# Gate projections of blocks 1 to 7: two blocks at a time in seven half-size products instead of eight

## The chip, the cores and the metric

The kernel runs on one core of a Trainium2 chip. The time is the device time of one execution in microseconds (us). Three runs of the kernel before took 754.03, 754.44 and 754.73 us. Engines: TensorE (PE, matmuls; its weight loads are shown apart as PEld), VectorE (DVE), ScalarE (ACT), GpSimd (POOL), and SyncE (SP), which issues the DMAs here. Each engine takes its instructions strictly in its own queue's order and waits at semaphores.

## The reference

A transformer block on 512 tokens of width 1024 in float32. After a normalization, one big projection gives the inputs of four mixers and, for each of them, a gate of full width:

```python
h = rmsnorm(x, norm_mix_pre[l])
(c_q, c_kv, k_r, sg_u, sg_v, cv_x, cv_b, cv_c, pool_in, gate_pre) = split_cols(h @ w_in[l])
gates = jax.nn.sigmoid(gate_pre + gate_b[l]).reshape(B_, S_, N_BRANCH, D_)
y_a = mla(...) @ w_br_mla[l]                  # attention
y_b = spatial_gating(...) @ w_br_sg[l]
y_c = short_conv(...) @ w_br_conv[l]
y_d = multiscale_pool(...) @ w_br_pool[l]
merged = (gates[:, :, 0] * y_a + gates[:, :, 1] * y_b
          + gates[:, :, 2] * y_c + gates[:, :, 3] * y_d)
x = x + rmsnorm(merged @ w_out[l], norm_mix_post[l])
h = rmsnorm(x, norm_ffn_pre[l])
f = jnp.square(jax.nn.relu(h @ w_ff1[l])) @ w_ff2[l]
x = x + rmsnorm(f, norm_ffn_post[l])
```

gate_pre has 4 x 1024 columns, so the gates are a product of [512, 1024] with [1024, 4096].

## The kernel before

Every float32 product is made of three matmuls: both operands are split into a high and a low half in a reduced-precision float32 format, and `mm3` (L119) adds hi x hi, hi x lo and lo x hi in PSUM. Weights come by DMA into a `raw` tile (three buffers, L105), ACT casts them to `wh` and DVE subtracts to get `wl` (L109 to L114; five buffers each). The activations z = x * g are split once into zh and zl, [128, 8, 512]: feature tile, token.

A gate block (`gate`, L431, by `feature_block`, L311) is 128 output columns: 8 K tiles x 3 matmuls of 128 rows x 512 tokens into one PSUM bank `fb`, then DVE multiplies with `rbc`, the tokens' inverse norms, into `g`. Block b needs four gates, one per mixer, and `merge(b)` (L438) applies the sigmoid on ACT, computes the four branch products `y` (24 matmuls with the weights wB), multiplies and adds on DVE and splits the sum into `mh` and `ml`, the output projection's operand. Eight blocks make the 1024 columns.

The order: first the low-rank projection, then the mixers. Attention's sixteen steps (four query tiles x four heads) are interleaved with the other mixers' feature blocks: `other()` (L461) advances a generator by one block, and when that is exhausted it computes one of block 0's four gates. After attention the loop at L659 computes gates and merges for blocks 0 to 7; the weights wO of the output projection (L703) follow in the same `raw` buffers. PE's instructions are issued in the order they are written in (L96); on the other engines a scheduler in the recording layer chose the order when the program was built, and it is fixed from then on. Tiles are given back and taken by pools; an instruction that writes a buffer waits for its last readers.

## Time and profile before

| | us |
|---|---|
| profiled execution, first to last instruction (span) | 754.0 |
| runs: lowest, median, highest | 754.03, 754.44, 754.73 |
| PE busy | 744.9 |
| DVE busy | 400.8 |
| ACT busy | 276.2 |
| POOL busy | 13.2 |
| merge of block 0 to the end of merge 7 | 152.21 to 349.60 |

The profiled execution's own time is not listed apart from the three runs; its span is 0.03 us under the lowest of them. Busy time is the time in which an engine has an instruction running. Matmuls overlap each other in the pipeline, so the mean duration of one (390 ns for 512 columns) is longer than the distance from one to the next; that distance is read from a stretch of known count.

### The profile page before, as it was taken

Reading aid. Unit: us, or ns where it says so; the run is one execution under the profiler, and the core shown is the slowest. Engines: PE = TensorE matmul, PEld = TensorE weight load, DVE = VectorE, ACT = ScalarE, POOL = GpSimd, SP = SyncE. Lnnn points to the kernel's source line nnn. Section 1 sums busy time; section 2 is a strip of 40 time slices with the busy share of each in tenths; the row PEclk is TensorE's granted clock in tenths of the full one; section 3 lists DMA queues with packets and bytes.
Section 4 is the critical chain, followed back from the end, with each engine's and each line's share of the span. In section 5 each row is a group of like instructions: output and inputs, shape, how many; then the busy total and the mean of one; then the engine's idle time right before and its main releaser. Section 6 shows DMA issues by size and latency. Waiting matters only on the chain.

```text
span 754.0 us, 8970 instructions
## 1 busy us (share of the span) xinstructions
PE 744.9 (99%) x3554; PEld 626.0 (83%) x3554; DVE 400.8 (53%) x673; ACT 276.2 (37%) x423; POOL 13.2 (2%) x28
## 2 busy tenths in 40 slices
PE   8999999999999999999999999999999999999996
PEld 8998888888888888888889888888888888888885
DVE  6599975366365455445376533343343334596624
ACT  5875443532232323232344522332332233321201
POOL 1110000000000000000000000000000000000001
PEclk9999999999999999999999999999999999999999
DMA  8433231272323222232204432223323223323203
GB/s 299 178 109 113 84 112 57 79 256 84 111 84 106 90 103 94 92 103 85 85 27 140 140 101 94 85 90 108 110 85 111 84 84 112 101 95 100 68 0 113
DMA packets 23146, 78.69 MB, mean 104 GB/s; under 512 B 3008, under 2 KB 3520, under 8 KB 23104
## 3 DMA queue, kind: packets, MB, share of 16 engines
q1 hardware_dynamic: 23072, 78.12, 31.0%
q8 instruction: 28, 0.46, 0.2%
q14 instruction: 14, 0.11, 0.1%
q0 software_dynamic: 32, 0.00, 0.0%
HBM read 76.01 MB, written 2.10 MB: 104 GB/s over the span
## 4 chain that ended last, share of the span: by engine, by line
PE 92%; DVE 5%; DMA 1%; ACT 1%; issue 0%; SPq 0%; DVEq 0%; ACTq 0%
PE fb L89 27%; PE z L89 23%; PE acc L89 23%; PE y L89 6%; PE wo L89 6%; PE psA L89 2%; PE sgv L89 2%; DMA xT<-in_xT 1%; DVE wl L113 1%; PE po L89 1%; DVE ql L531 1%; PE tr L89 1%; PE q L89 1%; PE s L89 0%; DVE m L590 0%
## 5 line engine op out<-in xcount | busy, mean ns | idle before, releaser
L89 ACT CAST wh<-raw 128x1024 fp32r<-128x1024 f32 (+1 forms) x126 | 131.7, 1047 | 366.3 <-PE z L89 148.4
L113 DVE TENSOR_TENSOR wl<-raw,wh 128x1024 fp32r<-128x1024 f32 (+1 forms) x126 | 153.1, 1217 | 158.2 <-ACT wh L89 157.0
L89 PE MATMUL fb<-zh,wh 128*128 128x512 f32 x336 | 131.6, 392 | 0.1
L89 PE MATMUL fb<-zh,wl 128*128 128x512 f32 x336 | 131.1, 390 | 0.0
L89 PE MATMUL fb<-zl,wh 128*128 128x512 f32 x336 | 130.8, 389 | 0.0
L89 PE MATMUL z<-hh,wh 128*128 128x512 f32 (+1 forms) x288 | 105.4, 366 | 0.0
L89 PE MATMUL z<-hl,wh 128*128 128x512 f32 (+1 forms) x288 | 105.3, 365 | 0.0
L89 PE MATMUL z<-hh,wl 128*128 128x512 f32 (+1 forms) x288 | 105.2, 365 | 0.0
L89 PE MATMUL acc<-wh,uh 128*128 128x512 f32 x232 | 90.2, 389 | 0.0
L89 PE MATMUL acc<-wl,uh 128*128 128x512 f32 x232 | 90.2, 389 | 0.0
L89 PE MATMUL acc<-wh,ul 128*128 128x512 f32 x232 | 90.2, 389 | 0.0
L89 PEld LDWEIGHTS fb<-zh,wl 128*128 128x128 f32 x336 | 63.0, 188 | 13.7 <-DVE wl L113 0.3
L89 PEld LDWEIGHTS fb<-zh,wh 128*128 128x128 f32 x336 | 63.1, 188 | 13.1 <-DVE zc L343 0.4
L89 PEld LDWEIGHTS fb<-zl,wh 128*128 128x128 f32 x336 | 63.1, 188 | 13.0
L434 DVE TENSOR_TENSOR g<-fb,rbc 128x512 f32<-128x512 f32 x32 | 22.1, 692 | 97.3 <-PE fb L89 97.3
L89 PEld LDWEIGHTS z<-hh,wl 128*128 128x128 f32 x288 | 54.3, 189 | 8.8
L89 PEld LDWEIGHTS z<-hl,wh 128*128 128x128 f32 x288 | 54.3, 189 | 8.7
L89 PEld LDWEIGHTS z<-hh,wh 128*128 128x128 f32 x288 | 54.3, 189 | 8.7
L89 PEld LDWEIGHTS acc<-wh,ul 128*128 128x128 f32 x232 | 43.5, 188 | 9.1
L89 PEld LDWEIGHTS acc<-wl,uh 128*128 128x128 f32 x232 | 43.5, 188 | 9.1
L89 PEld LDWEIGHTS acc<-wh,uh 128*128 128x128 f32 x232 | 43.5, 188 | 8.9
L751 DVE TENSOR_TENSOR ul<-u,uh 128x512 fp32r<-128x512 f32 x58 | 40.1, 692 | 3.2
(253 smaller groups left out, 852.8 us busy)
## 6 DMA issues: line engine op xcount, KB each, us to landing
raw<-in_w SPq DMA_DIRECT2D x64, 512.0 KB, 3.3
raw<-in_wG SPq DMA_DIRECT2D x32, 512.0 KB, 3.3
raw<-in_wF SPq DMA_DIRECT2D x10, 512.0 KB, 3.4
raw<-in_wB SPq DMA_DIRECT2D x8, 512.0 KB, 3.3
raw<-in_wO SPq DMA_DIRECT2D x8, 512.0 KB, 3.3
xk<-in_x SPq DMA_DIRECT2D x4, 512.0 KB, 10.1
x<-in_x SPq DMA_DIRECT2D x4, 512.0 KB, 5.8
out<-f SPq DMA_DIRECT2D x8, 256.0 KB, 2.0
```

Of the source, the lines that this page charges most:

```text
L89: ins = op(*a, **k)
L113: DVE.tensor_tensor(lo[:, :n], raw[:, :n], f(hi)[:, :n], ALU.subtract)
L434: DVE.tensor_tensor(g, ps, rbc, ALU.mult)
L531: DVE.tensor_tensor(dst[1][rows, :], src, f(dst[0])[rows, :], ALU.subtract)
L751: DVE.tensor_tensor(ul, uj, f(uh), ALU.subtract)
```

## The change

Blocks 1 to 7 compute their gates in pairs: gates 0 and 1, then gates 2 and 3 of a block. A pair is a product of [256 columns x 1024 features] with [1024 x 512 tokens]. Both are cut into four quarters (columns in two blocks of 128, features in two halves of 512, tokens in two halves of 256), and the 2 x 2 product of quarters is made in seven products of quarters instead of eight (Strassen's scheme in Winograd's form). One such product is 4 K tiles x 3 matmuls x 256 tokens = 12 matmuls. Sums that several outputs share stay in a PSUM bank, and later products are added on top of them (`more`), after ACT has copied the intermediate value out (`x`).

The scheme needs sums and differences of quarters. Those of z are made once, after attention: POOL adds zh + zl into two `quad` tiles, DVE combines, ACT and DVE split them into `sums_h` and `sums_l`; one more sum replaces the quarter (lower features, second tokens) of zh and zl themselves, after block 0's last gate has read them. Those of the weights are made per pair: one DMA of [128, 2048] (1 MB, two buffers) brings four quarters, POOL overwrites them with four differences between the casts, and seven quarter operands are split in tiles w1, w2, w3 (1024 wide) and w4 (512). The merge of the block before runs as `merge_steps` between the products of the pairs; its additions are on POOL instead of DVE.

Further: attention advances the other work at every third step instead of every second; the `raw` buffers move out of the permanent pool (three until attention ends, one during the blocks, three afterwards); x1, gmix and gffn are allocated and loaded after the merges; the larger mixer constants become a tile c2 of their own.

```diff
-    def mm3(ps, lhs, rhs, start, stop):
+    def mm3(ps, lhs, rhs, start, stop, more=False):
+        k = dict(skip_group_check=more)
...
-        raw = wp.tile([P, 1024], F32, tag="raw", name="raw", bufs=3)
+        raw = raws[0].tile([P, 1024], F32, tag="raw", name="raw", bufs=raws[1])
...
-        if i % 2 == 0:
+        if i % 3 == 0:
             other()
...
-    for b in range(KD):
-        while len(gates) < 4:
-            gates.append(gate(b, len(gates)))
-        merge(b)
+    raws[:] = [gw, 1]
+    def quad():
+        return gw.tile([P, 4 * 512], F32, tag="quad", name="quad", bufs=2)
+    for hh in range(2):
+        q = quad().rearrange("p (c k t) -> p c k t", c=4, k=2)
+        for c, (k, t) in enumerate(((0, 0), (HK, 0), (0, HS), (HK, HS))):
+            ix = slice(None), slice(k + 2 * hh, k + 2 * hh + 2), slice(t, t + HS)
+            POOL.tensor_tensor(q[:, c], f(zh)[ix], f(zl)[ix], ALU.add)
+        a11, a12, a21, a22 = (q[:, c] for c in range(4))
+        DVE.tensor_tensor(a22, a21, a22, ALU.add)
+        DVE.tensor_tensor(a21, a11, a21, ALU.subtract)
+        DVE.tensor_tensor(a11, a22, a11, ALU.subtract)
+        DVE.tensor_tensor(a12, a12, a11, ALU.subtract)
+        lower.append(a12)
+        ix = slice(None), slice(1, 3), slice(2 * hh, 2 * hh + 2)
+        ACT.copy(sums_h[ix], q[:, 2:])
+        DVE.tensor_tensor(sums_l[ix], q[:, 2:], f(sums_h)[ix], ALU.subtract)
+        ix = slice(None), 0, slice(2 * hh, 2 * hh + 2)
+        ACT.copy(sums_h[ix], a11)
+        DVE.tensor_tensor(sums_l[ix], a11, f(sums_h)[ix], ALU.subtract)
+    while len(gates) < 4:
+        gates.append(gate(0, len(gates)))
+    for hh in range(2):
+        ix = slice(None), slice(2 * hh, 2 * hh + 2), slice(HS, S)
+        ACT.copy(zh[ix], lower[hh])
+        DVE.tensor_tensor(zl[ix], lower[hh], f(zh)[ix], ALU.subtract)
...
+    def minus(q, out, a, b):
+        POOL.tensor_tensor(q[:, out * 512:(out + 1) * 512], q[:, a * 512:(a + 1) * 512], q[:, b * 512:(b + 1) * 512],
+                           ALU.subtract)
+    def pair(b, j):
+        q = quad()
+        nc.sync.dma_start(q, d["wS"][2 * (b - 1) + j])
+        w1 = split_w(q[:, :1024])
+        minus(q, 1, 2, 1)
+        minus(q, 2, 3, 2)
+        w2 = split_w(q[:, 512:1536])
+        minus(q, 1, 3, 1)
+        minus(q, 0, 0, 1)
+        w3 = split_w(q[:, :1024])
+        w4 = split_w(q[:, 1536:], 512)
+        def product(ps, w, at, a, first):
+            for k in range(HK):
+                mm3(ps[:, :HS], sl(w, slice(None), slice(at + k * P, at + (k + 1) * P)), sl(a, slice(None), k),
+                    first and k == 0, k == HK - 1, not first)
+        product(pa, w1, 512, A11, True)
+        ACT.copy(x1, pa[:, :HS])
+        yield
+        product(pb, w1, 0, A12, True)
+        DVE.tensor_tensor(g[0][:, :HS], pb[:, :HS], x1, ALU.add)
+        yield
+        product(pc, w2, 0, S1, True)
+        ACT.copy(x5, pc[:, :HS])
+        yield
+        product(pa, w3, 512, S2, False)
+        ACT.copy(x2, pa[:, :HS])
+        yield
+        product(pd, w3, 0, A22, True)
+        yield
+        product(pc, w4, 0, S4, False)
+        DVE.tensor_tensor(g[1][:, :HS], pc[:, :HS], x2, ALU.add)
+        yield
+        product(pa, w2, 512, S3, False)
+        ACT.copy(x3, pa[:, :HS])
+        DVE.tensor_tensor(g[0][:, HS:], pd[:, :HS], x3, ALU.add)
+        POOL.tensor_tensor(g[1][:, HS:], x3, x5, ALU.add)
+        for x in g:
+            DVE.tensor_tensor(x, x, rbc, ALU.mult)
...
+    for b in range(1, KD):
+        for j in range(2):
+            for n, _ in enumerate(pair(b, j)):
+                if (j or n >= 2) and n % 2 == 0:
+                    next(pending, None)
+        for _ in pending:
+            pass
+        pending = merge_steps(b)
...
+    raws[:] = [xp, 3]
...
         wo = [weights(d["wO"][hf, c]) for c in range(4)]
+        if hf == 0:
+            for t in range(NT):
+                nc.sync.dma_start(x1[:, t, :], d["x"][t * P:(t + 1) * P, :])
```

How the queues change at three places. First ACT inside the blocks. Before, in block 2 (wh are the weight casts, g the sigmoids, mh the merged block):

```order
L89 CAST wh_2060<-raw_2058 128x1024
L89 ACTIVATE g_1910<-g_1910,c1_62 128x512
L89 CAST wh_2093<-raw_2091 128x1024
L89 ACTIVATE g_1943<-g_1943,c1_62 128x512
L89 CAST wh_2126<-raw_2124 128x1024
L89 ACTIVATE g_1976<-g_1976,c1_62 128x512
L89 CAST wh_2159<-raw_2157 128x1024
L89 ACTIVATE g_2009<-g_2009,c1_62 128x512
L89 CAST wh_2196<-raw_2194 128x1024
L89 CAST mh_1651<-g_1910 128x512
```

Now, from the second pair of block 2 on: quad_2151 is that pair's weights, quad_2288 those of the first pair of block 3, pa, pc and x the PSUM banks and copies (2013 to 2019 of block 2's first pair, 2175 to 2181 of its second), mh that of block 1:

```order
L91 CAST wh_2159<-quad_2151 128x1024
L91 CAST wh_2165<-quad_2151 128x1024
L91 CAST wh_2169<-quad_2151 128x512
L91 COPY x_2018<-pa_2013 128x256
L91 ACTIVATE g_2012<-g_2012,c1_65 128x512
L91 COPY x_2178<-pa_2175 128x256
L91 ACTIVATE g_2011<-g_2011,c1_65 128x512
L91 CAST wh_2290<-quad_2288 128x1024
L91 CAST mh_1551<-g_1712 128x512
L91 COPY x_2181<-pc_2177 128x256
L91 CAST wh_2296<-quad_2288 128x1024
L91 COPY x_2179<-pa_2175 128x256
```

Casts and sigmoids alternated; now PSUM copies stand between casts of the next weights, and two of them (x_2181, x_2179) stand behind mh and behind a cast for the next pair.

Second, SP's queue where attention ends. Before (in_wG are gate weights, in_wB merge weights):

```order
L106 DMA raw_1561<-in_wG 128x1024
L106 DMA raw_1600<-in_wG 128x1024
L106 DMA raw_1657<-in_wB 128x1024
L106 DMA raw_1700<-in_wG 128x1024
L106 DMA raw_1733<-in_wG 128x1024
L106 DMA raw_1766<-in_wG 128x1024
```

Now (in_wS are the pairs' weights):

```order
L111 DMA raw_1506<-in_wG 128x1024
L111 DMA raw_1587<-in_wG 128x1024
L111 DMA raw_1620<-in_wG 128x1024
L111 DMA raw_1653<-in_wG 128x1024
L111 DMA raw_1764<-in_wB 128x1024
L702 DMA quad_1690<-in_wS 128x2048
L702 DMA quad_1852<-in_wS 128x2048
L702 DMA quad_1989<-in_wS 128x2048
L111 DMA raw_2063<-in_wB 128x1024
```

The small loads for block 1's gates are replaced by loads of 128x2048 into two quads, and these stand behind block 0's last gate and merge weights.

Third, ACT's queue where the output projection begins (raw<-in_wO give its weights; mh is the last block's). Before:

```order
L89 CAST wh_2974<-raw_2972 128x1024
L89 ACTIVATE g_2805<-g_2805,c1_62 128x512
L89 CAST wh_2980<-raw_2978 128x1024
L89 ACTIVATE g_2838<-g_2838,c1_62 128x512
L89 CAST wh_2986<-raw_2984 128x1024
L89 ACTIVATE g_2871<-g_2871,c1_62 128x512
L89 CAST wh_2992<-raw_2990 128x1024
L89 ACTIVATE g_2904<-g_2904,c1_62 128x512
L89 CAST wh_3114<-raw_3112 128x1024
L89 CAST mh_1651<-g_2805 128x512
```

Now:

```order
L91 ACTIVATE g_3669<-g_3669,c1_65 128x512
L91 ACTIVATE g_3668<-g_3668,c1_65 128x512
L91 CAST mh_1551<-g_3506 128x512
L91 CAST wh_3856<-raw_3854 128x1024
L91 CAST wh_3862<-raw_3860 128x1024
L91 CAST wh_3868<-raw_3866 128x1024
L91 CAST wh_3874<-raw_3872 128x1024
```

Three casts of the projection's weights, which stood between the last sigmoids, and a fourth now all come after the last mh.

## Rows read from the trace of the kernel before

**Rows 1.** The page: busy time and instructions; granted clock in 40 slices.

```profile
PE 744.9 (99%) x3554; PEld 626.0 (83%) x3554; DVE 400.8 (53%) x673; ACT 276.2 (37%) x423; POOL 13.2 (2%) x28
PEclk9999999999999999999999999999999999999999
```

**Rows 2.** The chain that ended last, in order of time: start us, us, what.

```profile
152.21 5.59 PE y L89 x24
157.80 21.80 PE fb L89 x96
179.60 5.60 PE y L89 x24
...
344.00 5.60 PE y L89 x24
349.60 33.59 PE wo L89 x144
...
397.01 8.63 PE z L89 x72
```

**Rows 3.** One block of gates and merge by engine: busy us (instructions), clock, DMA.

```profile
core 0: us, PE busy (x) PEld busy (x) DVE busy (x) ACT busy (x) POOL busy (x), PEclk, DMA share, GB/s
157.80:185.20 27.40, 27.40 (x121) 22.52 (x121) 14.14 (x18) 8.34 (x11) 0.00 (x0) 1.00 0.48 166
```

**Rows 4.** Groups by shape: count, busy us, mean ns, idle before and its releaser.

```profile
L89 ACT CAST wh<-raw 128x1024 fp32r<-128x1024 f32 x124 | 130.4, 1052 | 366.3 <-PE z L89 148.4 <-issue 106.6 <-PE acc L89 61.2
L89 ACT ACTIVATE g<-g,c 128x512 f32<-128x512 f32 x32 | 23.0, 718 | 0.0
L89 ACT CAST mh<-g 128x512 fp32r<-128x512 f32 x8 | 5.0, 620 | 6.0 <-DVE g L452 6.0
L89 ACT COPY pT<-pT 128x256 f32<-128x256 f32 x4 | 1.5, 369 | 0.8 <-PE pT L89 0.8
L89 ACT CAST wh<-raw 128x512 fp32r<-128x512 f32 x1 | 0.6, 616 | 0.0
...
L113 DVE TENSOR_TENSOR wl<-raw,wh 128x1024 fp32r<-128x1024 f32 x124 | 151.6, 1223 | 158.2 <-ACT wh L89 157.0 <-issue 0.3
L434 DVE TENSOR_TENSOR g<-fb,rbc 128x512 f32<-128x512 f32 x32 | 22.1, 692 | 97.3 <-PE fb L89 97.3
L628 DVE TENSOR_TENSOR al<-oT,ah 128x256 fp32r<-128x256 f32 x4 | 1.7, 418 | 0.2 <-ACT ah L89 0.2
L113 DVE TENSOR_TENSOR wl<-raw,wh 128x512 fp32r<-128x512 f32 x1 | 0.7, 687 | 0.0
```

**Rows 5.** Order of time: a gate's sigmoid and a weight split.

```profile
190.53 1.05 ACT L89 CAST wh<-raw 128x1024 fp32r<-128x1024 f32 x1 [3.23 <-PE fb L89]
191.49 0.72 ACT L89 ACTIVATE g<-g,c 128x512 f32<-128x512 f32 x1
191.62 1.23 DVE L113 TENSOR_TENSOR wl<-raw,wh 128x1024 fp32r<-128x1024 f32 x1 [0.21 <-ACT wh L89]
```

**Rows 6.** POOL in order of time: start us, us, operation, idle before.

```profile
2.40 0.30 POOL masks.py:199 TENSOR_SCALAR_AFFINE_SELECT ident<-ident 128x128 f32<-128x128 f32 x1
...
27.28 1.04 POOL L130 TENSOR_TENSOR rx<-ssx,nhalf 128x4 f32<-128x4 f32 x1 [24.01 <-DVE ssx L292]
28.59 0.63 POOL L335 TENSOR_SCALAR_AFFINE_SELECT wsg<-c 128x512 f32<-128x512 f32 x1
...
44.19 1.91 POOL L130 TENSOR_TENSOR rv<-rv,nhalf 128x4 f32<-128x4 f32 x1 [9.79 <-DVE rv L358]
...
392.57 0.54 POOL L130 TENSOR_TENSOR stt<-stt,nhalf 128x1 f32<-128x1 f32 x1 [5.92 <-DVE stt L682]
400.09 1.52 POOL L130 TENSOR_TENSOR stt<-stt,nhalf 128x1 f32<-128x1 f32 x1 [6.98 <-DVE r L701]
736.29 0.54 POOL L130 TENSOR_TENSOR sst<-sst,nhalf 128x1 f32<-128x1 f32 x1 [334.67 <-DVE sst L682]
```

**Rows 7.** DVE in order of time, beside three of POOL's operations.

```profile
44.02 1.22 DVE L113 TENSOR_TENSOR wl<-raw,wh 128x1024 fp32r<-128x1024 f32 x1
...
400.01 1.21 DVE L113 TENSOR_TENSOR wl<-raw,wh 128x1024 fp32r<-128x1024 f32 x1
...
736.06 0.74 DVE L816 SCALAR_TENSOR_TENSOR f<-acc,r,gpost 128x512 f32<-128x512 f32 x1
```

**Rows 8.** DMA issues: count, KB each, median us from issue to landing.

```profile
raw<-in_wG SPq DMA_DIRECT2D x32, 512.0 KB, 3.3
out<-f SPq DMA_DIRECT2D x8, 256.0 KB, 2.0
```

**Rows 9.** The last 14 us by stretch, columns as in rows 3.

```profile
740.00:748.00 8.00, 7.32 (x33) 5.73 (x31) 4.57 (x8) 1.06 (x3) 1.09 (x2) 1.00 0.35 130
748.00:750.00 2.00, 0.00 (x0) 0.00 (x0) 1.48 (x3) 0.49 (x2) 0.54 (x1) 1.00 0.04 9
750.00:752.00 2.00, 0.00 (x0) 0.00 (x0) 0.81 (x2) 0.00 (x0) 0.00 (x0) 0.82 0.50 187
752.00:754.00 2.00, 0.00 (x0) 0.00 (x0) 0.00 (x0) 0.00 (x0) 0.00 (x0) 0.50 0.20 75
```

**Rows 10.** PE in order of time at the beginning: first projection.

```profile
7.28 1.59 PE L89 MATMUL psA<-wah,zl 128*128 128x416 f32 x4
...
11.82 0.91 PE L89 MATMUL psA<-wal,zh 128*128 128x416 f32 x4
```

More of the change, by code (lines that the diff above doesn't have):

```diff
@@ L72 @@
 C1, NC1 = _cols(_C1)
+C2, NC2 = _cols(_C2)
 def build(ctx, tc, d, out):
@@ L303, in build @@
     bp = s3.enter_context(tc.tile_pool(name="bp", bufs=1, reuse_waits="tile"))
+    c2 = bp.tile([P, NC2], F32, name="c2")
+    nc.sync.dma_start(c2, d["c2"])
     def split(dst, j, src):
@@ L437, in build @@
     gates = []
-    def merge(b):
-        for i, g in enumerate(gates):
-            ACT.activation(g, g, AF.Sigmoid, bias=k1("gateb")[:, i * 8 + b:i * 8 + b + 1])
-        w = weights(d["wB"][b])
-        prev = None
-        for i, br in ((1, bT), (2, cT), (3, dT), (0, aT)):
-            g = gates[i]
-            ps = bank("y")
-            for k in range(2):
-                mm3(ps, sl(w, slice(None), slice((2 * i + k) * P, (2 * i + k + 1) * P)),
-                    sl(br, slice(None), k, slice(None)), k == 0, k == 1)
-            DVE.tensor_tensor(g, g, ps, ALU.mult)
-            if prev is not None:
-                DVE.tensor_tensor(g, g, prev, ALU.add)
-            prev = g
-        ACT.copy(mh[:, b, :], prev)
-        DVE.tensor_tensor(ml[:, b, :], prev, f(mh)[:, b, :], ALU.subtract)
-        gates.clear()
     others = branches()
@@ new lines, in build @@
+    sums_l = sp_.tile([P, 3, HK, HS], F32R, name="sums_l")
+    lower = []
+    for hh in range(2):
[15 more added lines that the diff above has]
+        DVE.tensor_tensor(sums_l[ix], a11, f(sums_h)[ix], ALU.subtract)
@@ new lines, in build @@
+    while len(gates) < 4:
[4 more added lines that the diff above has]
+        DVE.tensor_tensor(zl[ix], lower[hh], f(zh)[ix], ALU.subtract)
+    lo_k, hi_k, t0, t1 = slice(0, HK), slice(HK, KD), slice(0, HS), slice(HS, S)
+    A11, A12, A22 = (sl(z, slice(None), k, t) for k, t in ((lo_k, t0), (hi_k, t0), (hi_k, t1)))
+    S4 = sl(z, slice(None), lo_k, t1)
+    S2, S3, S1 = (sl((sums_h, sums_l), slice(None), c) for c in range(3))
@@ new lines, in small @@
+    def small():
+        return gw.tile([P, HS], F32, tag="x", name="x", bufs=6)
+    def minus(q, out, a, b):
[12 more added lines that the diff above has]
+        w4 = split_w(q[:, 1536:], 512)
+        g = [gp.tile([P, S], F32, tag="g", name="g", bufs=6) for _ in range(2)]
+        def product(ps, w, at, a, first):
+            for k in range(HK):
+                mm3(ps[:, :HS], sl(w, slice(None), slice(at + k * P, at + (k + 1) * P)), sl(a, slice(None), k),
+                    first and k == 0, k == HK - 1, not first)
+        pa, pb, pc = bank("pa"), bank("pb"), bank("pc")
+        x1, x2, x3, x5 = small(), small(), small(), small()
+        product(pa, w1, 512, A11, True)
[10 more added lines that the diff above has]
+        yield
+        pd = bank("pd")
+        product(pd, w3, 0, A22, True)
[9 more added lines that the diff above has]
+            DVE.tensor_tensor(x, x, rbc, ALU.mult)
+        gates.extend(g)
+        yield
@@ new lines, in merge_steps @@
+    def merge_steps(b):
+        gs = list(gates)
+        gates.clear()
+        for i, g in enumerate(gs):
+            ACT.activation(g, g, AF.Sigmoid, bias=k1("gateb")[:, i * 8 + b:i * 8 + b + 1])
+        w = weights(d["wB"][b])
+        prev = None
+        for i, br in ((1, bT), (2, cT), (3, dT), (0, aT)):
+            g = gs[i]
+            ps = bank("y")
+            for k in range(2):
+                mm3(ps, sl(w, slice(None), slice((2 * i + k) * P, (2 * i + k + 1) * P)),
+                    sl(br, slice(None), k, slice(None)), k == 0, k == 1)
+            DVE.tensor_tensor(g, g, ps, ALU.mult)
+            if prev is not None:
+                POOL.tensor_tensor(g, g, prev, ALU.add)
+            prev = g
+            if i:
+                yield
+        ACT.copy(mh[:, b, :], prev)
+        DVE.tensor_tensor(ml[:, b, :], prev, f(mh)[:, b, :], ALU.subtract)
+        yield
@@ new lines, in build @@
+    pending = merge_steps(0)
+    for b in range(1, KD):
[6 more added lines that the diff above has]
+        pending = merge_steps(b)
+    for _ in pending:
+        pass
+    s4.close()
+    s1.close()
+    xp = ctx.enter_context(tc.tile_pool(name="xp", bufs=1, reuse_waits="tile"))
+    raws[:] = [xp, 3]
+    x1 = xp.tile([P, NT, D], F32, name="x1")
@@ L663, in build @@
+    gmix = xp.tile([P, D], F32, name="gmix")
+    gffn = xp.tile([P, D], F32, name="gffn")
+    r2 = xp.tile([P, NT], F32, name="r2")
     nc.sync.dma_start(gmix, d["gmix"].partition_broadcast(P))
     nc.sync.dma_start(gffn, d["gffn"].partition_broadcast(P))
-    for t in range(NT):
-        nc.sync.dma_start(x1[:, t, :], d["x"][t * P:(t + 1) * P, :])
-    s1.close()
     hs = ExitStack()
@@ L882, in layout @@
     g["c1"] = c(np.concatenate([parts[k] for k in _C1], 1))
+    g["c2"] = c(np.concatenate([parts[k] for k in _C2], 1))
     return g
```

36 lines of the change are left out of this document (22 added, 14 removed).

## The prediction

> **What bounds the kernel now.** I read the busy times first: TensorE (PE) is busy for 744.9 of 754.0 us, and no slice of PEclk is under 9 [rows 1]. Next the chain that ended last, in order of time: from 152.21 us, where block 0's merge starts, to 349.60 us, where the output projection starts, it holds nothing but matmuls, seven times 21.80 us of gate products and 5.60 us of merge products; the projection's matmuls follow without a gap [rows 2]. Then one such block, 157.80 to 185.20 us, engine by engine: PE 27.40 of 27.40 us, DVE 14.14, ACT 8.34, POOL nothing, at clock 1.00 [rows 3]. So in the place of the change PE alone sets the pace, with half of DVE, two thirds of ACT and all of POOL to spare. A shorter PE stream gives its whole saving back as long as the other three can feed it; the question is whether they can.
>
> **What PE saves.** One block of gates is 96 matmuls of 512 columns in 21.80 us, 0.227 us each; the new form takes 84 matmuls of 256 columns per pair, 168 per block. The early FFN products of that width ran 72 in 8.63 us, 0.120 us each [rows 2]. A block goes from 21.80 to 168 x 0.120 = 20.14 us, with the merge from 27.40 to 25.74. Seven blocks: 7 x 1.66 = **11.6 us saved**. That is the most the change can give: an eighth fewer multiplications, of which the narrower matmul's larger fixed share takes back nearly half.
>
> **What the other engines get.** Durations [rows 4]: ACT's cast of 128x1024 weights 1.05 us (128x512: 0.62), DVE's split 1.22 (0.69), sigmoid 0.72, DVE 512-column elementwise 0.69, 256-column 0.42, ACT's 256-column copy out of PSUM 0.37, mh cast 0.62. From ACT's end to DVE's start, and back over POOL, I take 0.1 us: DVE's split at 191.62 us waited 0.21 us for the cast, of which most is the cast's own end [rows 5]. Per block DVE gets 8.7 us of pair splits, 1.2 of merge split, 2.5 of PSUM additions, 2.8 of rbc, 2.7 of merge multiplications and 0.7 of ml: 18.6 us. ACT gets 14. Both fit in 25.74. POOL gets eight weight differences, three merge additions and two half-size additions, twelve 512-column operations.
>
> POOL has no such row. The nearest below is its one-operand select: 128x512 in 0.63 us and 128x128 in 0.30, so 0.19 us and 0.86 ns a column [rows 6]. That is the lower end, since a second operand cannot make it cheaper. Two operands read one after the other give 0.19 + 512 x 1.72 ns = 1.07 us, two whole selects 1.26, the upper end. (The pow rows, 0.54 us for one column and 1.04 for four, time another function.) I take 1.07.
>
> POOL is also held up by DVE. A pow of one column takes 0.54 us at 392.57 [rows 6], but 1.52 when it starts at 400.09 beside a DVE weight split of 1.21 us that began at 400.01: it ends 0.39 after the split does. The four-column pow takes 1.04 alone and 1.91 beside the split at 44.02, ending 0.86 after it [rows 6, 7]. At 736.29 the pow runs 0.54 us beside a DVE instruction of 0.74 that reads one operand from PSUM [rows 6, 7]. So I let a POOL operation wait for a DVE instruction whose two operands are in SBUF, and the reverse.
> The Trainium skill (SBUF — State Buffer, "Who interferes with whom") has this as a rule: a DVE instruction with two SBUF inputs and a GpSimd one that reads SBUF exclude each other for a whole instruction, whichever issues first holding the port. The two slow pows agree; that DVE waits in turn for a two-operand POOL instruction no row here shows. The same skill (GPSIMD Engine Reference, "Elementwise — side-by-side cycle accounting") gives 4497 ns for a 2048-column add, by which an estimate for 512 is 1.12 us and the time about 4 us more than mine.
>
> **The order decides.** The queues run in program order, so I walk one block of the second kind (merge of block 1 beside pair (2,1)), t = 0 at the end of a block's last product. A pair's weights go through one chain: cast w1, split, two differences on POOL that overwrite half of the quad, cast w2, split, two differences, cast w3 and w4, splits. In ACT's queue the casts stand between PSUM copies that PE waits for.
> - Cast w2 of the first pair ended at -1.85 (shown below to close). Split to -0.6, differences to 1.65, casts w3, w4, wB to 4.45, their splits to 5.9. The first merge product needs wB's low half at 5.9, where PE could use it at 4.8: the pair ends at 14.0 (12.9 without waits).
> - DVE then does one addition, waits for POOL's half-size addition (held by wB's split) to 6.55, rbc to 7.9, an addition, and w1's split of the second pair to 9.5. Differences to 11.75, cast w2 to 12.9, split to 14.2, differences to 16.4, casts w3, w4 and the last copy of the first pair to 18.55, split w3 to 18.8, half-size addition to 19.45, rbc to 20.8, a merge multiplication, split w4 to 22.15.
> - ACT: two sigmoids and a copy to 22.0, cast w1 of block 3's first pair to 23.05. DVE splits it 23.2 to 24.4. POOL's last merge addition, held by that, ends at 25.5, and the mh cast behind it at 26.2. Behind mh stands the copy of product 3 (26.6), which PE needs before it may add product 6 to that bank. PE was there at 24.0, waits 2.7 us, ends product 6 at 28.1.
> - Two differences (with ml's subtraction between) to 28.3, cast w2 of block 3's first pair 29.45, which is again 1.85 before the end; the copy behind it 29.8, product 7 waits 1.8 us and ends at **31.3**.
>
> So a block takes 31.3 us, set by the ring cast, split, difference and merge addition, and not by PE's 25.74. Six blocks: 6 x 5.56 = 33.4; block 1's second pair 2.4; the last pair, with no successor to prepare, gives back 1.7: **34.1 us lost**.
>
> **Start.** In-attention gates go from four to one, three move behind it: PE has the same work up to the first pair, so t = 0 here is the first moved gate. DVE's queue has eight instructions of the sums ahead of that gate's split (6.9 us), so it ends at 11.9 instead of 5.45; one raw buffer (512 KB land in 3.3 us [rows 8]) makes the next two end at 17.6 and 23.3, not 16.35. Then nothing covers the first pair: quad 0 is free only after zh's quarter has been rewritten behind the last gate (24.8), 1 MB lands 5.5 us later (an estimate from 256 KB in 2.0 and 512 KB in 3.3 [rows 8]; 4.6 to 7.6), cast 31.4. w2, w3 and wB go through the ring with PE waiting: the first merge product ends at 44.7, the pair at 51.9 instead of 29.2: **22.7 us lost**. In attention each score and its transpose still have a feature block between them; I cost it at nothing (0 to 2 if that cover is thin).
>
> **End.** The second wO raw buffer lies over aT or the gates and waits for the last merge product; the first cast stands behind mh. From the last pair's end: gate additions, rbc, sigmoids, merge ends on ACT at 8.3, first cast 9.4, split 10.7, chunks paced by 3.3 us of landing, cast and split: the first projection tile ends at 17.6 instead of 11.0: **6.6 us lost**. x1's loads are no longer early, but are needed only in the second half.
>
> **Clock.** PE's last matmul here ends at 747.3 (busy 7.32 us from 740 on); the granted clock is 1.00 to 750, 0.82 in 750 to 752 and 0.50 (1.2 GHz) in 752 to 754 [rows 9]. The 8 us of the start would do the same; four matmuls of 416 columns took 1.59 us at the beginning and 0.91 at 11.82 [rows 10], so some 12 such matmuls cost 2 us (0 to 4). **2 us lost.**
>
> **Sum.** 754.0 - 11.6 + 22.7 + 34.1 + 6.6 + 2.0 = 807.8. The span shown is 754.0, the runs 754.03 to 754.73, median 0.4 above the span: **808 us**.
>
> **Rivals.**
> 1. POOL is cheap. With 0.63 us per operation the ring closes in 26.5 us, start 20.5, end 5.3: 775 us. With 1.07 and no exclusion it closes in 29.0: 792. For it: POOL's selects are quick. Against: two operands, and the slow pows. Chance 0.30 for all between 765 and 795.
> 2. The clock falls inside the blocks too. PE at 1.2 GHz would need 51 us a block: up to 940 us. Against: the waits are 2.7 and 1.8 us, and with no matmul since 747.3 the clock still stood at 1.00 to 750 [rows 9]. Chance 0.07 for over 830.
> 3. Everything is fed, so that PE's saving arrives: 754.0 - 11.6 = 742.4 us. It decides if start and end together lose less than 11.6 and the ring closes under 25.74. For it: DVE's and ACT's sums fit, POOL was empty. Against: the start alone waits for 1 MB behind the last gate (7.5 us), the end for wO. Chance 0.05, part of it no change.
> The forecast (795 to 830) has 0.58.
>
> **Numbers.** 808 us, range 774 to 828, which the two ends of POOL's price (775 and 821) fill. What repeated runs of this kernel can tell apart is 0.2%: faster 0.03, same 0.02, slower 0.95.
>
> **What would show it.** Right: PE idle 5 to 9 us before the first pair; a block of 29 to 33 us; PE waiting in the second pairs for ACT copies that stand behind mh and behind a quad cast; POOL subtractions longer beside weight splits; the first projection tile late by 5 to 8 us. Wrong: blocks near 25.7 us, or a subtraction near 0.6 us, or a clock under 1.00 through the blocks.

## The result, and the profile after

The changed kernel takes **827.61 us** (median of 4 runs, 827.15 to 828.37) where the kernel before took 754.59 (754.03 to 754.86): a ratio of 1.0969, 95% interval 1.0953 to 1.0985. It is slower, as forecast, by 73 us where 53 were forecast. The profiled execution has a span of 826.2 us. The page, to be held against [rows 1]:

```profile
PE 767.1 (93%) x4058; PEld 654.4 (79%) x4058; DVE 439.9 (53%) x733; ACT 315.1 (38%) x511; POOL 155.7 (19%) x130
PEclk9998999869999899899899999999999999999998
```

PE's share fell from 99% to 93%, and POOL went from 13.2 to 155.7 us. The granted clock fell after PE's waits in attention, in the start, at the end of the blocks and in single blocks. The chain that ended last, in order of time, shows what bounds it now (to [rows 2]; start us, us, what):

```profile
164.35 4.74 DMA quad<-in_wS
...
264.93 2.13 POOL g L763
267.06 1.24 POOL quad L696
268.36 1.62 POOL quad L696
270.01 1.05 ACT wh L91
271.09 1.24 DVE wl L118
272.39 1.29 POOL quad L696
273.75 1.28 POOL quad L696
275.03 2.86 issue
277.92 1.79 POOL g L742
280.35 0.69 DVE g L744
281.37 1.14 DVE wl L118
...
295.34 1.11 POOL g L763
297.04 2.12 POOL g L763
...
497.78 5.60 PE z L91 x24
503.38 2.80 PE acc L91 x12
```

Where the chain of the kernel before held nothing but matmuls, no matmul stands between 264.93 and 297.04: POOL's differences and sums (L696, L742, L763), ACT's cast, DVE's split, and round again. The 2.86 us of "issue" belong to the ring too: POOL waits there for ACT's copy x, and in ACT's queue that copy stands behind three casts of weights (275.06 to 277.57):

```profile
277.92 1.78 POOL L742 TENSOR_TENSOR g<-x 128x256 f32<-128x256 f32 x1 [2.90 <-ACT x L91]
```

From one block's last merge addition on POOL (264.93) to the next block's (297.04) it is 32.11 us: that is the block's time. Two blocks and a stretch of attention by engine (to [rows 3]):

```profile
core 0: us, PE busy (x) PEld busy (x) DVE busy (x) ACT busy (x) POOL busy (x), PEclk, DMA share, GB/s
232.81:264.93 32.12, 26.88 (x194) 24.64 (x193) 17.87 (x25) 13.52 (x22) 18.35 (x13) 1.00 0.24 83
264.93:297.04 32.11, 28.91 (x194) 27.12 (x193) 17.89 (x25) 13.62 (x22) 18.34 (x14) 0.89 0.23 83
...
60.00:90.00 30.00, 25.41 (x130) 20.31 (x130) 28.04 (x50) 15.85 (x26) 0.11 (x1) 0.89 0.38 124
```

No engine is full in a block: POOL, the new one, is busy for 18.4 of 32.1 us. What fills the time is the ring, not an engine. In the second block the clock fell to 0.89 and the block was no longer: PE only waited less. In attention, where the kernel before has PE busy for all of 30.00 us, PE now stands 4.6 us: the transpose of the first score's softmax p waits 4.52 us for it, and the clock falls after that. The same stretch of the kernel before, then that transpose, and last the same p in the kernel before, where a second feature block stood ahead of the transpose:

```profile
60.00:90.00 30.00, 30.00 (x162) 24.04 (x160) 29.43 (x53) 16.83 (x27) 0.11 (x1) 1.00 0.37 124
```

```profile
80.01 1.11 PE L91 MATMUL pT<-ident,p 128*128 128x128 f32 x4 [4.52 <-ACT p L91]
```

```profile
78.90 0.69 ACT L89 ACTIVATE p<-s,m 128x512 f32<-128x512 f32 x1
```

PE's longest waits in a block of the changed kernel, in order of time:

```profile
235.91 0.39 PE L91 MATMUL pc<-zh,wh 128*128 128x256 f32 x1 [1.95 <-ACT x L91]
...
239.25 0.38 PE L91 MATMUL pa<-sums_h,wh 128*128 128x256 f32 x1 [1.65 <-ACT x L91]
```

They are the two that the walk ended with, before the copies behind mh and behind the next pair's cast (2.7 and 1.8 us there). The groups by shape behind it (to [rows 4]):

```profile
L91 PE MATMUL acc<-wh,uh 128*128 128x512 f32 x232 | 91.8, 396 | 0.0
...
L91 PE MATMUL z<-hh,wh 128*128 128x512 f32 x224 | 88.4, 395 | 0.0
L696 POOL TENSOR_TENSOR quad<-quad 128x512 f32<-128x512 f32 x56 | 74.0, 1321 | 89.0 <-DVE wl L118 86.8
...
L118 DVE TENSOR_TENSOR wl<-quad,wh 128x1024 fp32r<-128x1024 f32 x42 | 52.6, 1253 | 87.3 <-ACT wh L91 87.3
...
L763 POOL TENSOR_TENSOR g<-g 128x512 f32<-128x512 f32 x24 | 39.1, 1631 | 18.1 <-DVE g L761 17.4
...
L742 POOL TENSOR_TENSOR g<-x 128x256 f32<-128x256 f32 x14 | 18.3, 1306 | 26.9 <-ACT x L91 26.9
```

A 512-column difference takes 1.32 us on POOL (1.07 was taken), a merge addition 1.63: 1.30 alone, and 2.13 in the chain's row at 264.93, which began beside a DVE weight split (264.51 to 265.94). The 256-column addition (L742) takes 0.99 alone and 1.78 beside a split. The first two groups belong to the FFN, which the change doesn't touch: in the kernel before they have means of 389 ns.

Span to span, 826.2 - 754.0 = 72.2 us, against the terms of the forecast (the runs differ by 73.0; a run's time is some 1.7 us above its span, 827.95 against 826.2, where the forecast allowed 0.4):

| term | forecast us | measured us | where it is read |
|---|---|---|---|
| PE's saving | -11.6 | -11.6 | carried over, not measured in this kernel; a fed block takes 25.70 us in experiment 12 (25.74 forecast) |
| attention | 0 to 2 | +6.3 | PE is free for the first moved gate at 142.18; before, 135.86 (152.21 less three gates of 5.45) |
| start (clock with it) | +24.7 | +21.8 | from there to the end of the first pair, 193.19, 51.0 us; 29.2 for the same work fed (16.35 + 12.87) |
| blocks | +34.1 | +39.1 | a block of 32.1 us, not 31.3 |
| end | +6.6 | +7.7 | end of the last pair (399.58) to the start of the second projection tile (418.33) 18.75 us, before 11.03 |
| FFN and rest | 0 | +8.9 | from there to the last instruction 407.9 us, before 399.0; z x24 5.60 us, before 5.44; acc x12 2.80, before 2.72 |
| sum | 53.8 | 72.2 | |

### The profile page after: what moved, and what is told of

The parts are those of the page before. It is cut to its first block, busy times and chain, and to the rows that moved or that the text cites. A ratio compares the mean times of both kernels' runs of the same rounds, so it can differ in the third digit from the quotient of the medians.

```text
span 826.2 us, 10275 instructions
## 1 busy us (share of the span) xinstructions
PE 767.1 (93%) x4058; PEld 654.4 (79%) x4058; DVE 439.9 (53%) x733; ACT 315.1 (38%) x511; POOL 155.7 (19%) x130
## 4 chain that ended last, share of the span: by engine, by line
PE 65%; POOL 14%; DVE 8%; ACT 5%; issue 4%; DMA 2%; SPq 0%; DVEq 0%; POOLq 0%; ACTq 0%
PE acc L91 22%; PE z L91 22%; POOL quad L696 9%; PE fb L91 7%; PE wo L91 6%; ACT wh L91 4%; DVE wl L118 4%; POOL g L763 3%; PE psA L91 2%; POOL g L742 2%; PE sgv L91 1%; DVE g L744 1%; PE po L91 1%; PE s L91 1%; PE pT L91 1%
## 5 line engine op out<-in xcount | busy, mean ns | idle before, releaser
L118 DVE TENSOR_TENSOR wl<-raw,wh 128x1024 fp32r<-128x1024 f32 (+1 forms) x98 | 118.8, 1216 | 164.6 <-ACT wh L91 163.4
L91 ACT CAST wh<-raw 128x1024 fp32r<-128x1024 f32 (+1 forms) x98 | 101.8, 1043 | 234.3 <-PE z L91 153.5
L118 DVE TENSOR_TENSOR wl<-quad,wh 128x1024 fp32r<-128x1024 f32 (+1 forms) x56 | 61.6, 1111 | 87.3 <-ACT wh L91 87.3
L696 POOL TENSOR_TENSOR quad<-quad 128x512 f32<-128x512 f32 x56 | 74.0, 1321 | 89.0 <-DVE wl L118 86.8
L91 ACT CAST wh<-quad 128x1024 fp32r<-128x1024 f32 (+1 forms) x56 | 51.3, 941 | 89.5 <-POOL quad L696 87.9
L136 POOL TENSOR_TENSOR sst<-sst,nhalf 128x1 f32<-128x1 f32 x4 | 2.2, 550 | 354.3 <-DVE sst L807 354.3
L91 PEld LDWEIGHTS acc<-wh,uh 128*128 128x128 f32 x232 | 43.6, 188 | 10.7
L91 PE MATMUL fb<-zh,wh 128*128 128x512 f32 x112 | 45.4, 405 | 3.3 <-ACT wh L91 3.3
L91 PE MATMUL fb<-zh,wl 128*128 128x512 f32 x112 | 45.0, 401 | 2.7 <-DVE wl L118 2.7
L91 PE MATMUL fb<-zl,wh 128*128 128x512 f32 x112 | 44.8, 400 | 0.0
L91 PE MATMUL pa<-sums_h,wh 128*128 128x256 f32 x112 | 34.3, 306 | 10.1 <-ACT x L91 10.1
```

Of the source, the lines that this page charges most:

```text
L91: ins = op(*a, **k)
L118: DVE.tensor_tensor(lo[:, :n], raw[:, :n], f(hi)[:, :n], ALU.subtract)
L136: POOL.tensor_tensor(dst, src, nhalf[:, :n], ALU.pow)
L696: POOL.tensor_tensor(q[:, out * 512:(out + 1) * 512], q[:, a * 512:(a + 1) * 512], q[:, b * 512:(b + 1) * 512], ALU.subtract)
```

## The experiments

Each ran beside the kernel before; ratios are to it, with their 95% intervals. Experiments 1, 2, 3, 5 and 6 ask where the FFN's 9 us come from, since that part is computed by the same instructions; they are numbered in the order of the runs.

**1. Operands placed at multiples of 128 or 256 bytes, in the kernel before.**

```
     cs = zp.tile([P, 2, NT, 16], F32, name="cs")
+    zp.tile([P, 24], F32, name="pad0")
...
     ml = mpool.tile([P, KD, S], F32R, name="ml")
+    mpool.tile([P, 16], F32, name="pad1")
```

> The kernel before, with two unused tiles that move the mixers' outputs (aT to dT) and mh, ml to addresses in SBUF that are multiples of 128 bytes; nothing else is changed. Theory (the address of a matmul's operands sets its pace): in before, fb, z and acc, whose operands all start at multiples of 128, go at 0.2267 us per 512-column matmul, y (moving operand at 32 modulo 128) and wo (stationary operand at 64) at 0.2333. y and wo should fall to 0.2267, each 192 matmuls: 2 x 1.28 us, so 754.6 to 752.0 (751.4 to 752.4). Rival (y and wo are slower for what they are: their operands, their order or their engines' neighbours): 754.6, y x24 and wo x24 still 5.60 us.

It took 753.02 us, ratio 0.9976 (0.9967 to 0.9986). The chain:

```profile
315.18 5.59 PE y L89 x24
...
348.14 32.66 PE wo L89 x144
```

The output projection went from 33.59 to 32.66 us with mh and ml at 128 beyond a multiple of 256; the merge products stayed at 5.59, with aT to dT at a multiple of 256 itself. So place matters, but "a multiple of 128" is not the rule.

**2. The FFN's operands moved off their place, in the kernel before.**

```
     hp_ = hs.enter_context(tc.tile_pool(name="hp", bufs=1, reuse_waits="tile"))
+    hp_.tile([P, 16], F32, name="pad0")
...
     sst = up.tile([P, NT, 4], F32, name="sst")
+    up.tile([P, 24], F32, name="pad1")
```

> The kernel before, with two unused tiles that move hh, hl to 64 and uh, ul to 32 modulo 128 bytes. Theory (addresses): acc goes from 0.2267 to 0.2333 us per matmul as in the changed kernel, 12 matmuls 2.80 instead of 2.72 us; z too if 64 counts as off for the moving operand as it does for wo's stationary one (24 matmuls 5.60 instead of 5.44). With both 754.6 + 9.2 = 763.8, with acc alone 754.6 + 4.6 = 759.2. Rival (the feed-forward part of the changed kernel is slower for another reason, such as a clock or the loads beside it): 754.6, no change.

761.5 us, ratio 1.0091 (1.0078 to 1.0105): z x24 took 5.50 us and acc x12 2.81. Nothing but addresses changed, and the kernel before is 7 us slower, between the two values expected: hh and hl, moved by 64 bytes, lost only part of what the other pair lost.

**3. Four pads in the changed kernel, two of them shown.**

```
     r2 = xp.tile([P, NT], F32, name="r2")
+    xp.tile([P, 24], F32, name="pad2")
...
     sst = up.tile([P, NT, 4], F32, name="sst")
+    up.tile([P, 8], F32, name="pad3")
```

> The changed kernel, with four unused tiles that move its mixers' outputs, sums, quads, mh, ml, hh, hl, uh and ul to multiples of 128 bytes. Theory (addresses): the feed-forward part goes back to 5.44 and 2.72 us per 24 and 12 matmuls and gives 9.2 us, wo 1.3; in the blocks PE is not what bounds, so 827.6 to 817 (816 to 818). Rival (another reason): 827.6.

821.8 us, ratio 1.0889 (1.0874 to 1.0904), with pad0 and pad1 of 24 elements. The chain has `501.82 2.74 PE acc` (uh now at 128 modulo 256, as the weights) but still `496.23 5.59 PE z` (hh at 0). It gave back 5.8 us, in acc and in the output projection (wo x24 5.63 to 5.49, mh now at 128 too): again only where the place equals that of the weights. z, at 0, gave back nothing.

**5. In the kernel before, aT to dT, mh and ml put at the weights' place modulo 256.**

```
+    zp.tile([P, 56], F32, name="pad0")
...
+    mpool.tile([P, 16], F32, name="pad1")
```

> The kernel before, with unused tiles that move aT to dT and mh, ml to 128 modulo 256 bytes, where wh and wl stand (36480 and so on). Theory (a 512-column matmul goes at 0.2267 us where its moving and its stationary operand start at the same place modulo 256 bytes, at up to 0.2333 elsewhere): y falls from 5.60 to 5.44 per 24, which moving the same tiles to 0 modulo 256 did not bring, and wo to 5.46: 8 x 0.16 + 8 x 0.14 = 2.4 us, 754.6 to 752.2. Rival (y is slower for another reason): y stays at 5.60 and the time at 753.0, as with b_aligned.

751.96 us, ratio 0.9961 (0.9948 to 0.9973): **faster than both kernels**, by pads alone. The chain:

```profile
341.63 5.44 PE y L89 x24
347.07 32.64 PE wo L89 x144
```

**6. The weights moved by 32 bytes, in the kernel before (a single run).**

```
     wp = ctx.enter_context(tc.tile_pool(name="wp", bufs=1))
+    wp.tile([P, 8], F32, name="pad0")
```

> The kernel before, with 32 unused bytes ahead of wh: wh, wl, zh, zl, hh and hl all move to 160 modulo 256, uh and ul stay at 128. Theory (the two operands' places against each other count): fb and z stay at 5.44 per 24 matmuls although both their operands have moved, acc rises to 2.80 per 12 although uh and ul have not: 754.6 + 4.6 = 759. Rival (each operand's own place counts): fb, z and acc all rise, by 0.16 per 24 matmuls, 754.6 + 13 = 768.

760.01 us. The chain:

```profile
434.41 5.45 PE z L89 x24
439.85 2.79 PE acc L89 x12
```

uh kept its address and acc went from 2.72 to 2.79; the pool's shift moved z's and the gates' operands along with the weights, and those kept their pace. So it is the place of the two operands to each other, modulo 256 bytes, that counts: operands that agree modulo 128 alone were slow (y in experiment 1), and uh, which agrees with the weights modulo 256 and not modulo 512, was fast. In the kernel before, weights, zh, hh and uh all stand at 128; in the changed one the weights and zh do, while other pools ahead of them put hh and uh at 160 and mh at 224 (192 before; the branch tiles are at 160 in both). In experiments 11 and 12, changed kernels with all of these at 128, z is back at 5.44 and acc at 2.72. That is the 9 us of the FFN and rest.

The other seven test the ring, the start and attention in the changed kernel.

**4. No differences.**

```
-        minus(q, 1, 2, 1)
-        minus(q, 2, 3, 2)
         w2 = split_w(q[:, 512:1536])
-        minus(q, 1, 3, 1)
-        minus(q, 0, 0, 1)
```

> The changed kernel without the four weight differences of each pair (w2 and w3 are cast from the quad as it was loaded, so the gates of blocks 1 to 7 are other numbers). Theory (the ring cast, split, POOL difference sets the block): a block falls from 32.1 us to PE's 25.7 to 26.5, six blocks give 34 to 38 us, the start some 5 to 7 (four differences of 1.3 us with PE waiting, the last pairs 2 to 3): 827.6 to 779 to 787. Rival (the order of ACT's queue, copies behind mh and casts, or DVE's sum holds PE, with POOL merely beside it): a block stays above 30 us and the time above 812.

782.03 us, ratio 1.0362 (1.0348 to 1.0376), within the forecast of the ring. A block:

```profile
202.84:228.84 26.00, 25.85 (x194) 24.56 (x193) 18.15 (x25) 13.86 (x23) 7.12 (x5) 1.00 0.27 101
```

26.00 us, PE busy for 25.85 of them: without POOL's eight differences a block has PE's pace. Leaving them out gives back 45.6 us of the 73, 37.8 in the thirteen pairs after the first and 6.8 in the start. It takes away the ring and eight of POOL's operations at once, so it does not tell the two apart.

**7. The differences out of place, so that no cast waits for another's split.**

```
-        return gw.tile([P, 4 * 512], F32, tag="quad", name="quad", bufs=2)
+        return gw.tile([P, 4 * 512], F32, tag=tag, name=tag)
...
+        e = quad("diff")
+        minus(part(e, 2), part(q, 2), part(q, 1))
+        minus(part(e, 3), part(q, 3), part(q, 2))
+        minus(part(e, 1), part(q, 3), part(e, 2))
+        minus(part(e, 0), part(q, 0), part(e, 1))
         w1 = split_w(q[:, :1024])
...
+        w2 = split_w(e[:, 1024:])
+        w3 = split_w(e[:, :1024])
```

> The changed kernel, its differences written to a tile of their own (diff, one buffer, beside quad with one buffer) instead of over the quad, so that the four follow each other without a cast or split between; the sums of z use the same two tiles. Theory (the ring through cast, split and difference is too long, not POOL's work of 1.3 us per difference): a load of 4.8 us, four differences of 1.3 to 1.6 us and the splits of w1 and w4 take 11 us for the quad, under a pair's 13.0, so a block falls from 32.1 to 26 to 27.5 us, the start by 3 to 5: 827.6 to 786 to 796. Rival (POOL itself with its exclusion is too slow beside DVE's splits): a block stays above 30, 815 or more.

819.55 us, ratio 1.086 (1.0844 to 1.0877): the rival's number. A block, and two groups:

```profile
199.38:230.97 31.59, 26.64 (x192) 24.59 (x192) 20.74 (x25) 13.64 (x22) 20.05 (x14) 1.00 0.24 84
```

```profile
L699 POOL TENSOR_TENSOR diff<-quad,diff 128x512 f32<-128x512 f32 x28 | 54.1, 1933 | 1.1
...
L118 DVE TENSOR_TENSOR wl<-quad,wh 128x1024 fp32r<-128x1024 f32 x14 | 24.6, 1760 | 17.1 <-ACT wh L91 17.1
```

The ring through the splits was open and the block lost half a microsecond. Set free from each other, POOL's later differences (1.3 us alone) take 1.93 and DVE's split of w1 (1.22) 1.76: each now waits for the other inside its own duration. But the edit also left one quad instead of two, and POOL's first difference of a pair now waits for the load:

```profile
L699 POOL TENSOR_TENSOR diff<-quad 128x512 f32<-128x512 f32 x28 | 45.9, 1664 | 60.8 <-DMA quad<-in_wS 60.8
```

That is 4.3 us a pair, 8.7 a block, beside POOL's 20.05 busy: the rival's number came with a second cause, and how much of the 31.59 is exclusion alone is not shown. An estimate from the durations: per block POOL has eleven 512-column operations of 1.30 us and two of 256 columns of 0.99, 16.3 us, and DVE 13.4 us of instructions with both operands in SBUF (pair splits 8.7, merge split 1.2, rbc 2.8, ml 0.7). If these always exclude each other they fill 29.7 us, more than PE's 25.7, and then no order could have fed PE with this work on POOL. No run tests that without the wait for the load.

**9. As 7, with the differences on DVE.**

```
-        POOL.tensor_tensor(out, a, b, ALU.subtract)
+        DVE.tensor_tensor(out, a, b, ALU.subtract)
```

> As a_out_of_place (differences written to a tile of their own), but the four differences of a pair on DVE instead of POOL; POOL keeps the merge's additions. Theory (POOL's two-operand instructions and DVE's instructions with both operands in SBUF exclude each other, so a block needs their sum: eight differences and four other operations of about 1.3 us beside 13 us of DVE's splits, rbc and ml, 29 us): on DVE a difference costs 0.69, the sum falls to 25 us and DVE's own work rises to 24, so a block takes 26 to 27.5 us instead of 31.0, 819.6 to 786 to 795. Rival (DVE, in its own order, becomes the bound in POOL's place): a block stays above 29.5, 808 or more.

804.58 us, ratio 1.0671 (1.0654 to 1.0687), above the 786 to 795 expected, in the right direction. A block:

```profile
197.00:225.86 28.86, 26.45 (x195) 24.57 (x194) 22.21 (x32) 13.47 (x23) 7.05 (x5) 1.00 0.25 92
```

Against experiment 7, where only the engine of the differences is another, a block falls by 2.7 us: eight more instructions on DVE are cheaper than on POOL. PE still waits 1.1 to 2.0 us for a split in the order that the queues happen to have.

**8. Attention's cover moved to where a transpose would wait.**

```
-        if i % 3 == 0:
+        if i in (0, 2) or i % 3 == 2:
             other()
```

> The changed kernel, with attention's other work at steps 0, 2, 5, 8 and so on instead of 0, 3, 6, 9: eight blocks as now. Theory (the 6.3 us that attention lost are one transpose at 75 us that waits 4.5 us for its softmax, which stands behind the splits of q in DVE's queue, and TensorE's lower clock after it): the block now at step 2 covers that wait, 827.6 to 821.5 (820.5 to 823). Rival (attention is late because DVE is late as a whole, or another step waits in its place): 826 or more.

825.56 us, ratio 1.0934 (1.0916 to 1.0953), 4 us above the expectation. The first score's transpose no longer waits (79.80); the third score's, at attention's step 4, now does:

```profile
84.31 0.66 PE L91 MATMUL pT<-ident,p 128*128 128x128 f32 x4 [2.19 <-ACT p L91]
```

Attention ended at 138.35, 3.8 us earlier; the whole gained 2.05. The start gave 1.0 back: from attention's end to the end of the first pair it is 52.0 us instead of 51.0. PE's waits there are 13.7 us in both, but of the 20.5 us at 1.2 GHz that the start has in both, PE is busy for 16.9 here and for 14.8 in the changed kernel, which is the 1.0 us. The rest of the difference is not taken apart.

**10. The first pair's weights loaded ahead of the gates, and the gates put ahead of the sums.**

```
+    first, first_e = (fpool.tile([P, 4 * 512], F32, name=n) for n in ("first", "first_e"))
...
     lower = []
+    nc.sync.dma_start(first, d["wS"][0])
+    while len(gates) < 4:
+        gates.append(gate(0, len(gates)))
```

> The changed kernel with its start alone altered: the first pair's 1 MB goes to a tile over what becomes ml later, issued ahead of block 0's moved gates, and these gates stand ahead of the sums of z in the program. Theory (the start's loss is a chain: sums, gates, quad free, 4.8 us of load, then the ring with nothing beside it): the load and most of the first ring go under the gates, the first pair ends 35 to 39 us after attention instead of 51.0; 827.6 to 812 to 816. Rival (the start is held by DVE's and POOL's work on the sums, wherever the load stands): above 822.

824.09 us, ratio 1.0928 (1.091 to 1.0946): the rival's number. The first pair ends 47.2 us after attention, not 35 to 39. The 4.7 us of loading are hidden, but the moved gate at 147.26 waits 5.78 us for its cast and 1.79 for its split. ACT's and DVE's queues are ordered by the scheduler and still hold the sums' casts and additions ahead, and these wait for POOL.

**11. Everything so far together** (7, 9, 10, a better cover, all operands at the weights' place, half of the wO weights split early):

```
-        if i % 3 == 0:
+        if i in (0, 2, 4) or i > 4 and i % 3 == 1:
...
+    wo0 = []
+    for n, t in enumerate(("quad", "diff")):
+        q = quad(t)
+        for c in range(2):
+            raw = q[:, c * 1024:(c + 1) * 1024]
+            nc.sync.dma_start(raw, d["wO"][0, 2 * n + c])
+            wo0.append(split_w(raw))
```

> All together: differences on DVE in a tile of their own, the first pair's load ahead of the gates, other work of attention at steps 0, 2, 4, 7, 10 and so on, two raw buffers in the blocks, the first half of the output projection's weights loaded into quad and diff ahead of the last merge, and every operand of the 512-column products at 128 modulo 256 bytes. Theory: 754.6 - 11.6 (fewer multiplications) - 2.4 (places) + 0 to 2 (attention) + 4 to 8 (start) + 0 to 9 (blocks of 25.7 to 27) + 0 to 2 (end) + 1 (clock): 748 to 762, likeliest 752. Rival (DVE at 24 of 26 us with its waits bounds the blocks): 765 or more.

769.01 us, ratio 1.0192 (1.0177 to 1.0208): above the forecast, the rival's number, but not for the rival's reason. Blocks take 26.9 us, as forecast; the start lost 14.3 us (4 to 8 forecast), since its wait for the cast grew to 9.14, and the end 4.8 (0 to 2). DVE and ACT in the start, in order of time:

```profile
140.64 1.73 DVE L683 TENSOR_TENSOR quad<-quad 128x512 f32<-128x512 f32 x1 [4.16 <-POOL quad L681]
...
144.07 1.04 ACT L91 CAST sums_h<-quad 128x1024 fp32r<-128x1024 f32 x1 [6.69 <-DVE quad L684]
145.03 1.04 ACT L91 CAST wh<-raw 128x1024 fp32r<-128x1024 f32 x1
```

The gate's cast stands behind the sums' cast, that behind DVE's sums, and these behind POOL's. The first sum takes 1.73 us where 512 columns otherwise take 0.69.

**12. As 11, with the start and the blocks in an order written by hand on ACT and DVE, no POOL in the blocks, and four of the eight sums on DVE.**

```
-    PE, ACT = InOrder(nc.tensor, True), InOrder(nc.scalar, False)
+    PE, ACT, DVE = InOrder(nc.tensor, True), InOrder(nc.scalar, False), InOrder(nc.vector, False)
...
+    def half():
+        return gw.tile([P, 2 * 512], F32, tag="half", name="half", bufs=3)
...
+    ZE = [[POOL] * 4, [DVE] * 4]
...
+    zsum(0)
+    feed(1)
+    feed_at(2, first_e[:, :1024])
+    feed_at(3, first_e[:, 1024:])
+    zsum(1)
+    gates.append(gate(0, 1))
+    pre.append(prep_first())
```

> As a_combined, with POOL out of the blocks and the order written by hand: the merge's additions and the half-size additions are on DVE too (POOL keeps four of the eight sums zh + zl), ACT's and DVE's instructions from the moved gates to the last merge are kept in the order they are written in, each next weight operand is prepared as soon as a buffer is free, the pair's load comes in two halves (three buffers), and attention's other work is at steps 0, 2, 5, 8 and so on. Theory (POOL's instructions and DVE's with both operands in SBUF exclude each other, and the scheduler's order adds the waits; DVE alone has 24 us of work a block by its measured spacing of 0.60, 1.13 and 0.34 us, TensorE 25.4): a block takes 25.4 to 26 us instead of a_combined's 26.9, the start loses 5 instead of 11 us: 746 to 752, likeliest 748, faster than before. Rival (DVE with all of it is the bound, each wait for TensorE in its queue costs TensorE too): a block stays at 26.5 or more and the time at 757 or more.

755.57 us, ratio 1.0010 (1.0002 to 1.0019): neither the 746 to 752 expected nor the rival's 757 and more. A block, and attention with the start:

```profile
195.70:221.40 25.70, 25.70 (x194) 24.67 (x193) 24.49 (x38) 14.16 (x23) 0.00 (x0) 1.00 0.29 103
...
60.00:90.00 30.00, 27.61 (x148) 22.42 (x147) 29.27 (x53) 15.67 (x25) 0.11 (x1) 0.94 0.36 124
...
120.00:150.00 30.00, 24.65 (x108) 19.45 (x107) 20.30 (x32) 7.87 (x15) 3.93 (x3) 0.85 0.34 123
```

The block is full: PE 25.70 of 25.70 us, DVE 24.49. So PE's saving is real, and it is eaten elsewhere: by 2.39 us of waits in attention (at 84.47), 5.35 at the moved gate (143.28), and a granted clock of half speed, 1.2 GHz, after these waits, in which PE is busy for 10.7 us, about 5.3 us of work at full speed. With 0.9 us at the end that is 13.9, against 11.9 of saving (seven blocks of 25.70 us for 27.40) and 1.0 from mh's better place; the difference of 1.0 is near the 0.9 measured. That an order exists which keeps the saving is not shown.

## Why the prediction was right, and where it was not

- **Direction and mechanism: right.** The ring cast, split, difference and merge addition set the block: the chain shows it, experiment 4 takes it away, and PE waits in the second pairs where the walk put its waits. The size was near the edge: 827.6 lies 0.4 us inside the range, whose upper end was a dear POOL, while 15 us came from two terms that stood at nothing (below). That it stayed inside is luck.
- **POOL's price: too low.** 1.07 us was taken from selects; one takes 1.30, above the "two whole selects" of 1.26 that stood as upper end. A bound from another function is no bound. That the block came out only 0.8 above the walked 31.3 is partly luck: by a straight line through the forecast's own 26.5 us (at 0.63) and 31.3 (at 1.07), 1.30 would give 33.8, so another piece of the walk was too long, and which is open. PE's waits in a block are 5.2 us (3.6 in the two long ones), where the walk had 5.6 (4.5); PE is busy for 26.9 us, where the same work takes 25.7 fed: after each wait the first matmul of 256 columns takes 0.39 us instead of 0.28, and the last one before it has no successor to overlap it.
- **Exclusion: right, and now in both directions.** The forecast let a POOL operation wait for DVE's split and the reverse, and named the second unseen. Experiment 7's rows show it: split 1.76 us, not 1.22. The Trainium skill (SBUF — State Buffer, "Who interferes with whom") has the rule, and the trace agrees. What was not drawn from it is the sum over a block, 29.7 us by the estimate at experiment 7, which alone would say "not fed". By the estimate from the Trainium skill (GPSIMD Engine Reference, "Elementwise — side-by-side cycle accounting"), an operation would take 1.12 us; 1.30 was measured.
- **Start: the sum right within 3 us, the parts not.** The forecast was 22.7 us of waits and 2.0 of clock; measured are 13.7 of waits (3.33 and 2.65 at the moved gate, 3.25 and 0.46 at the first pair, 4.01 at its first merge product) and a clock at 1.2 GHz for 20.5 us, of which PE is busy for 14.8: 7.4 us of work. Before the first pair PE stood 3.25 us, not the 5 to 9 named as a sign. The quad lands in 4.74 us (5.5 taken), and earlier, 26.9 us after the first moved gate and not 30.3. Two errors of opposite sign made the sum, which is luck. Experiments 10 and 11 show why waits remain: the gate's cast stands behind work that waits for POOL. How much of it an order alone can remove isn't settled; experiment 12 leaves 5.35 us.
- **End: right in size** (7.7, 6.6 forecast), again with other parts: PE waits 4.7 us for the first cast and split, and the clock at 1.2 GHz, from 408.7 to 415.5, makes up the rest; no clock was forecast there.
- **Clock: too low, and in too few places.** 2 us were forecast, for the start. It is about 7 there, 2 in attention behind the wait of 4.52 us, and 3 at the end. In single blocks it fell at no cost.
- **The step that failed: "In attention each score and its transpose still have a feature block between them; I cost it at nothing."** It cost 6.3 us: a wait of 4.52 and the slower clock behind it. The sentence is true and not enough. One block in three steps instead of two leaves steps 2 and 4 without a block of their own, where the first and the third score's transposes stand (experiment 8 covers the first, and then the third waits). The trace of before had the number: its first p ends at 79.59, and PE without the block that began at 75.35 would have stood there for 4.2 us.
- **The step that was missing: the FFN.** It was taken to be untouched, and it is, by instruction. The tiles' places are not: 8.9 us (experiments 2, 3, 5, 6, 11 and 12). With it and attention the forecast would have been 823.
- **Rivals.** POOL cheap: fell, 1.30 us. The clock in the blocks: fell as a cost. Everything is fed: only the blocks of experiments 4 and 12 are, and in 12 DVE has 24.49 of 25.70 us. The ring against the mere sum of POOL's and DVE's work: not told apart, since the run that opened the ring (7) brought a wait for the load.

## What to carry to other kernels

A scheme that saves multiplications pays in additions on the other engines; before the walk through the queues, add per stage what two engines may not do at once (here POOL and DVE on SBUF) and hold it against PE's time. A saving of 1.5% is smaller than what its edges cost: cover in the stage before, the start and the end of the pipeline, and the clock after each wait. And when pools change, compare the SBUF places of operands of matmuls that are not touched.
